# Residual halves side by side in one 512-column matmul, and weight sums formed by accumulating DMAs, in a seven-product SwiGLU stage

## The chip, the core and the metric

The kernel runs on one core of one Trainium2 chip. The metric is the device time of one launch in microseconds (us). The kernel before was run three times: 2362.85 us is the median, 2361.63 and 2367.12 the lowest and highest. A separate execution was recorded by the hardware profiler; it took 2364.33 us, of which 2362.6 us lie between the first and the last instruction (the span).

## The reference

The reference is one encoder layer over 512 tokens (two requests of 256), model width 2048: a mixing part (attention and a gated delta rule), a residual, and then a SwiGLU block whose inner width is 5632. The change touches the last line only, in the two products with `w_gate` and `w_up`:

```python
    h = h + mixed
    hn = rmsnorm(h, norm_ffn_w)
    return h + (jax.nn.silu(hn @ w_gate) * (hn @ w_up)) @ w_down
```

Everything is float32. The kernel gets that accuracy on TensorE by splitting each operand into a high part (rounded to float32r) and a low part (the rest), and adding three products: high weight with high activation, high weight with low activation, low weight with high activation.

## The kernel before

The gate and up products are computed with a seven-product scheme of Strassen's kind. The contraction (2048 rows) is cut in two halves, the 256 + 256 tokens are the two column halves, and two neighbouring blocks of 128 output columns are the two row halves. Seven sums of activation blocks (`A11, A12, S4, A22, S1, S2, S3`, 256 tokens each) are made once, ahead of the stage, for each of eight k-tiles (lines 846 to 857); `split` at line 857 writes their high parts to `XH[k]` and their low parts to `XL[k]`. On the weight side, sums of blocks are made for every block.

The stage is the loop at line 956: 22 pairs, each with one `block` of the gate weights and one of the up weights, so 44 calls of `block` (line 883). One call:

- loads four weight blocks of 128 x 1024 float32 (512 KB each) through SyncE's queue (`b11`, `b12` in a pool of their own for gate and for up, one buffer each; `b22`, `b21` in the three `raw` buffers);
- makes the sums of weights it needs with four VectorE operations (lines 905, 909, 915, 927);
- splits each of the seven weight operands (`w_split`, lines 874 to 878): ScalarE writes the high part `w_hi` (line 123), VectorE the low part `w_lo` (line 124), each in one of three rotating buffers;
- runs seven products (`product`, lines 866 to 872), each of 8 k-tiles times 3 matmuls of 256 columns;
- combines the products out of PSUM: ScalarE copies (lines 903, 913, 935), VectorE additions (919, 924, 925, 932), a multiplication by the reciprocal norm (937).

After an up block VectorE multiplies up and gate (963), and GpSimd's queue stores the result to `s_act` (971), which the last stage (`w_down`, 512-column matmuls throughout) loads again as `raw_a`.

Each engine works through its own instructions in a fixed order. The matmuls stay in program order. On the other engines a scheduler sets the order when the kernel is built; `ahead()` lets it place the weight splits some way ahead of the product that uses them.

The output columns of one `product` are half a PSUM bank, so products share banks: `pa` and `pc` hold two each.

Of the kernel before, what the change touches and what calls it, by code (L numbers as in the profile page):

```python
# [8 lines left out]
F32 = mybir.dt.float32  # L9
F32R = mybir.dt.float32r  # L10
I32 = mybir.dt.int32
AF = mybir.ActivationFunctionType
ALU = mybir.AluOpType
# [4 lines left out]
P = 128  # L18
T = 512
# [4 lines left out]
L = 256  # L24
# [29 lines left out]
def r32(ap):  # L54
    return ap.bitcast(F32)
# [3 lines left out]
def hybrid_encoder(ctx: ExitStack, tc: tile.TileContext, xT, w_in, w_ba, w_out, w_gate,  # L59
                   w_up, w_down, nw_mix, nw_ffn, nw_fin, na_bias, conv_w, lane_par,  # L60
                   dn_nw, y):
    nc = tc.nc
    act = nc.scalar.activation
    tt = nc.vector.tensor_tensor
# [5 lines left out]
    def mm(*a, **k):  # L70
        pin(nc.tensor.matmul(*a, **k))  # L71
# [6 lines left out]
    wp = ctx.enter_context(tc.tile_pool(name="wp", bufs=2, side="left"))  # L78
# [5 lines left out]
    pg = ctx.enter_context(tc.tile_pool(name="pg", bufs=3, space=PSUM))  # L84
# [35 lines left out]
    def split(hi, lo, src, scale=None):  # L120

        if scale is None:
            act(out=hi, in_=src, func=AF.Copy)  # L123
            tt(lo, src, r32(hi), ALU.subtract)  # L124
        else:
            act(out=hi, in_=src, func=AF.Copy, scale=scale)
            stt(lo, src, scale, r32(hi), ALU.mult, ALU.subtract)
# [50 lines left out]
    def half_gemm(ps, src, xs, start, stop, every=2):  # L178

        wh, wl = load_w(src, [8, P])  # L180
        for k in range(8):
            mm3(ps, wh[:, k], wl[:, k], xs[k][0], xs[k][1],
                start and k == 0, stop and k == 7)
            if k % every == every - 1:
                pump()
        advance(vector_work)

    def col_tile(src, xs):
        ps = pg.tile([P, T], F32, tag="g", name="ps_g")
        half_gemm(ps, src[0], xs[:8], True, False)  # L190
        half_gemm(ps, src[1], xs[8:], False, True)
        return ps
# [17 lines left out]
    psm = ctx.enter_context(tc.tile_pool(name="psm", bufs=3, space=PSUM))  # L210
    pso = ctx.enter_context(tc.tile_pool(name="pso", bufs=1, space=PSUM))
# [57 lines left out]
    for j in range(8):  # L269
        for k in (2 * j, 2 * j + 1):  # L270
            wh, wl = k0w[k // 8]
# [257 lines left out]
    for h in range(H):  # L529
        kq = wk.tile([P, 2, T], F32, tag="kq", bufs=2, name="kq")  # L530
        ps = ps_k0 if h == 0 else col_tile(w_in[2 * h], xs)
        conv_silu(ps, 8 + h, kq[:, 0])
        ps = ps_q0 if h == 0 else col_tile(w_in[2 * h + 1], xs)
# [62 lines left out]
    for h in range(H):  # L596
        ps = col_tile(w_in[16 + 3 * h], xs)
        qT = na.tile([P, T], F32, tag="qT", name="qT")
        stt(qT, ps, QSCALE, rstd, ALU.mult, ALU.mult)
        ps = col_tile(w_in[16 + 3 * h + 1], xs)  # L600
        kT = evac(ps, "kT", 1, na)
        ps = col_tile(w_in[16 + 3 * h + 2], xs)
# [168 lines left out]
    for h in range(H):  # L771
# [6 lines left out]
        ps = col_tile(w_in[40 + 2 * h], xs)  # L778
# [3 lines left out]
        ps = col_tile(w_in[40 + 2 * h + 1], xs)  # L782
# [29 lines left out]
    for i in pairs:  # L812
        ps = pg.tile([P, T], F32, tag="g", name="ps_g")
# [11 lines left out]

    hp_cm = tc.tile_pool(name="hp", bufs=1, side="right", reuse_waits="tile")
    hp = hp_cm.__enter__()
    XH = [hp.tile([P, 7, L], F32R, tag=f"xh{k}", name="xch") for k in range(8)]
    XL = [hp.tile([P, 7, L], F32R, tag=f"xl{k}", name="xcl") for k in range(8)]
    ga_cm = tc.tile_pool(name="gA", bufs=1, side="right", reuse_waits="tile")  # L830
    gA = ga_cm.__enter__()
    st_cm = tc.tile_pool(name="st", bufs=1, side="left", reuse_waits="tile")
# [2 lines left out]
    A11, A12, S4, A22, S1, S2, S3 = range(7)  # L835
    for n, i in enumerate(pairs):
        j = i % 8
        ps = pg.tile([P, T], F32, tag="g", name="ps_g")
        hk = st.tile([P, T], F32, tag="hk", bufs=2, name="hk")
        nc.sync.dma_start(hk, s_h1[i])  # L840
        half_gemm(ps, w_out[i, 1], dns, True, True)
        tt(hk, hk, ps, ALU.add)
        nc.gpsimd.dma_start(s_h2[i], hk)
        w = nwf[:, i:i + 1]
        if i < 8:
            cmb = st.tile([P, 7, L], F32, tag="cmb", name="cmb")
            a21 = st.tile([P, L], F32, tag="a21", name="a21")
            act(out=cmb[:, A11], in_=hk[:, :L], func=AF.Copy, scale=w)
            act(out=a21, in_=hk[:, L:], func=AF.Copy, scale=w)
            tt(cmb[:, S3], cmb[:, A11], a21, ALU.subtract)  # L850
        else:
            act(out=cmb[:, A12], in_=hk[:, :L], func=AF.Copy, scale=w)
            act(out=cmb[:, A22], in_=hk[:, L:], func=AF.Copy, scale=w)
            tt(cmb[:, S1], a21, cmb[:, A22], ALU.add)
            tt(cmb[:, S2], cmb[:, S1], cmb[:, A11], ALU.subtract)
            tt(cmb[:, S4], cmb[:, A12], cmb[:, S2], ALU.subtract)
            split(XH[j], XL[j], cmb)
        sq = acc if n == 0 else st.tile([P, T], F32, tag="sq", name="h_sq")
        act(out=sq, in_=hk, func=AF.Square)
        if n:  # L860
            tt(acc, acc, sq, ALU.add)
# [4 lines left out]
    def product(ps, w, c, first, done=False):  # L866

        wh, wl = w
        for k in range(8):
            for n, (u, x) in enumerate(((wh, XH), (wh, XL), (wl, XH))):  # L870
                mm(ps, u[:, k], x[k][:, c], start=(first and k == 0 and n == 0),
                   stop=(done and k == 7 and n == 2), skip_group_check=True)

    def w_split(src):
        hi = wp.tile([P, 8, P], F32R, tag="hi", bufs=3, name="w_hi")
        lo = wp.tile([P, 8, P], F32R, tag="lo", bufs=3, name="w_lo")
        split(hi, lo, src)
        return hi, lo

    def ahead():  # L880
        return tc.high_priority(offset=AHEAD)

    def block(src, f, pool, new_out, opened=None):

        with tc.high_priority(offset=3 * AHEAD):
            b11 = pool.tile([P, 8, P], F32, tag="b11", name="b11")
            b12 = pool.tile([P, 8, P], F32, tag="b12", name="b12")
            nc.sync.dma_start(b11, src[f, 0])
            nc.sync.dma_start(b12, src[f + 1, 0])
            b22 = wp.tile([P, 8, P], F32, tag="raw", bufs=3, name="b22")  # L890
            nc.sync.dma_start(b22, src[f + 1, 1])
            b21 = wp.tile([P, 8, P], F32, tag="raw", bufs=3, name="b21")
            nc.sync.dma_start(b21, src[f, 1])
        pa = pg.tile([P, T], F32, tag="g", name="ps_a")
        pc = psm.tile([P, T], F32, tag="s", name="ps_c")
        with ahead():
            w = w_split(b11)
        product(pa[:, :L], w, A11, True)
        if opened:
            opened()  # L900
        fp, out = state["fp"], new_out()
        p1 = fp.tile([P, L], F32, tag="p1", bufs=2, name="p1")
        nc.scalar.copy(p1, pa[:, :L])
        with ahead():
            tt(b11, b12, b11, ALU.subtract)
            w = w_split(b11)
        product(pc[:, L:], w, S1, True)
        with ahead():
            tt(b12, b22, b12, ALU.subtract)
            w = w_split(b12)  # L910
        product(pc[:, :L], w, S3, False)
        p75 = fp.tile([P, 2, L], F32, tag="p75", bufs=2, name="p75")
        nc.scalar.copy(p75, pc.rearrange("p (a t) -> p a t", a=2))
        with ahead():
            tt(b11, b22, b11, ALU.subtract)
            w = w_split(b11)
        product(pa[:, L:], w, S2, False)
        u2 = fp.tile([P, L], F32, tag="u2", bufs=2, name="u2")
        tt(u2, p1, pa[:, L:], ALU.add)
        with ahead():  # L920
            w = w_split(b22)
        product(pc[:, L:], w, S4, False, True)
        v = fp.tile([P, L], F32, tag="v", name="v")
        tt(v, u2, p75[:, 0], ALU.add)
        tt(out[:, 3], v, p75[:, 1], ALU.add)
        with ahead():
            tt(b11, b21, b11, ALU.subtract)
            w = w_split(b11)
        product(pc[:, :L], w, A22, False, True)
        with ahead():  # L930
            w = w_split(b21)
        tt(out[:, 1:3], pc.rearrange("p (a t) -> p a t", a=2),
           u2[:, None, :].broadcast_to([P, 2, L]), ALU.add)
        product(pa[:, :L], w, A12, False, True)
        nc.scalar.copy(out[:, 0], pa[:, :L])
        a = out.rearrange("p (f b) t -> p f (b t)", f=2)
        tt(a, a, rstd2[:, None, :].broadcast_to([P, 2, T]), ALU.mult)  # L937
        return out
# [17 lines left out]
    for p in range(NPAIR):  # L956
# [8 lines left out]
        if p // 2 == FIRST_SEG:  # L965
            k = p % 2 * 2
# [21 lines left out]
    fp = ctx.enter_context(tc.tile_pool(name="fq", bufs=2, side="left", reuse_waits="tile"))  # L988
# [174 lines left out]
```

## Time and profile before

| What | us |
|---|---|
| median of three runs | 2362.85 |
| the profiled execution, own time | 2364.33 |
| its span | 2362.6 |
| PE busy in the span | 2323.2 |
| VectorE busy | 1599.0 |
| ScalarE busy | 975.0 |
| GpSimd busy | 143.8 |
| the 20 loads of `raw_a` by GpSimd's queue, median from issue to landing | 4.6 |

In the profile PE is TensorE's matmul side, PEld its weight loads, DVE VectorE, ACT ScalarE, POOL GpSimd, SP SyncE, which issues DMAs. A row of a group has the line of the kernel, engine, operation, output and inputs, shape and count; then busy time, the mean of one in ns, and the idle time of the engine just before them with what ended it. A row of the timeline has start and duration in us and, in brackets, the idle time before it. A matmul's duration in the trace reaches from its start to the end of its pipeline, so that neighbours overlap; the distance from one start to the next is what counts for throughput.

### The profile page before, as it was taken

The page shows a single profiled execution, that of the slowest core. Times are in us where ns is not written, and L with a number is a line of the kernel's source. Part 1 is how long each engine was busy: PE and PEld are TensorE (multiplying, and loading weights), DVE is VectorE, ACT ScalarE, POOL GpSimd, SP SyncE. Part 2 cuts the span into 40 slices and gives each one's busy share as a digit, 9 for nine tenths or more (in the row PEclk, how much of TensorE's full clock was granted, in tenths as well). Part 3 has the DMA queues.
Part 4 walks back from the last instruction along what each step waited for, and adds up shares of the span by engine and source line. Part 5 has one row for each costly group of instructions (what it writes and reads, how often), then busy time and mean ns, then how long its engine had stood idle before and what let it go on. Part 6 is the DMA issues. An engine that isn't in the chain of part 4 may idle for free.

```text
span 2362.6 us, 35608 instructions
## 1 busy us (share of the span) xinstructions
PE 2323.2 (98%) x14500; PEld 2058.6 (87%) x14500; DVE 1599.0 (68%) x2164; ACT 975.0 (41%) x1464; POOL 143.8 (6%) x244
## 2 busy tenths in 40 slices
PE   8999999999999999899999999999999999999997
PEld 6777788877778788799999999999999888888887
DVE  7644699985566637788888888888888653422346
ACT  6777223324333315544444444444444331211125
POOL 2111200002100001000000000000000110000000
PEclk9999999999999999999999999999999999999999
DMA  5434623346434546333333333333333563423332
GB/s 202 130 116 132 161 93 103 95 120 179 145 115 125 212 157 208 120 115 119 116 126 117 126 117 119 114 121 113 118 106 99 192 227 98 133 93 97 98 125 72
DMA packets 88980, 305.30 MB, mean 129 GB/s; under 512 B 11776, under 2 KB 16288, under 8 KB 87664
## 3 DMA queue, kind: packets, MB, share of 16 engines
q1 hardware_dynamic: 71392, 245.67, 32.5%
q0 software_dynamic: 17424, 57.36, 8.0%
q8 instruction: 114, 1.87, 0.3%
q14 instruction: 50, 0.41, 0.1%
HBM read 266.98 MB, written 36.00 MB: 128 GB/s over the span
## 4 chain that ended last, share of the span: by engine, by line
PE 57%; DVE 0%; DMA 0%; issue 0%; ACT 0%; POOL 0%; DVEq 0%
PE ps_c L71 21%; PE ps_a L71 16%; PE ps_g L71 11%; PE ps_s L71 9%; DMA raw_a<-s_act 0%; DVE hT L1043 0%; DVE w_lo L124 0%; DVE up L937 0%; ACT w_hi L123 0%; ACT aq L123 0%; DVE up L963 0%; DVE hT L1010 0%; DVE dgs L1037 0%; POOL s_act L971 0%; DVE ssq_acc L1060 0%
## 5 line engine op out<-in xcount | busy, mean ns | idle before, releaser
L123 ACT ACTIVATE w_hi<-b 128x1024 fp32r<-128x1024 f32 x308 | 327.0, 1062 | 490.9 <-PE ps_c L71 164.6
L124 DVE TENSOR_TENSOR w_lo<-w_raw,w_hi 128x1024 fp32r<-128x1024 f32 x224 | 274.1, 1224 | 277.9 <-ACT w_hi L123 273.9
L124 DVE TENSOR_TENSOR w_lo<-b,w_hi 128x1024 fp32r<-128x1024 f32 x308 | 376.3, 1222 | 120.3 <-ACT w_hi L123 120.3
L123 ACT ACTIVATE w_hi<-w_raw 128x1024 fp32r<-128x1024 f32 x224 | 236.8, 1058 | 487.0 <-PE ps_s L71 278.2
L71 PE MATMUL ps_c<-xch,w_hi 128*128 128x256 f32 x1408 | 399.9, 284 | 0.0
L71 PE MATMUL ps_c<-xcl,w_hi 128*128 128x256 f32 x1408 | 399.0, 283 | 0.0
L71 PE MATMUL ps_c<-xch,w_lo 128*128 128x256 f32 x1408 | 399.0, 283 | 0.0
L71 PE MATMUL ps_g<-xhi,w_hi 128*128 128x512 f32 x896 | 369.6, 412 | 0.0
L71 PE MATMUL ps_g<-xhi,w_lo 128*128 128x512 f32 x896 | 351.6, 392 | 6.6 <-DVE w_lo L124 6.6
L71 PE MATMUL ps_g<-xlo,w_hi 128*128 128x512 f32 x896 | 350.8, 392 | 0.0
L71 PE MATMUL ps_a<-xch,w_hi 128*128 128x256 f32 x1056 | 299.0, 283 | 5.3 <-ACT xch L123 4.0
L71 PE MATMUL ps_a<-xcl,w_hi 128*128 128x256 f32 x1056 | 299.1, 283 | 1.7 <-DVE xcl L124 1.7
L71 PE MATMUL ps_a<-xch,w_lo 128*128 128x256 f32 x1056 | 299.0, 283 | 0.0
L71 PEld LDWEIGHTS ps_c<-xch,w_hi 128*128 128x128 f32 x1408 | 271.0, 192 | 0.5 <-issue 0.5
L71 PEld LDWEIGHTS ps_c<-xcl,w_hi 128*128 128x128 f32 x1408 | 271.0, 192 | 0.5 <-issue 0.5
L71 PEld LDWEIGHTS ps_c<-xch,w_lo 128*128 128x128 f32 x1408 | 270.9, 192 | 0.0
L71 PEld LDWEIGHTS ps_g<-xhi,w_lo 128*128 128x128 f32 x896 | 168.8, 188 | 46.0 <-DVE w_lo L124 9.1
L71 PEld LDWEIGHTS ps_a<-xch,w_hi 128*128 128x128 f32 x1056 | 202.7, 192 | 5.7 <-ACT xch L123 4.2
L71 PEld LDWEIGHTS ps_g<-xhi,w_hi 128*128 128x128 f32 x896 | 169.0, 189 | 43.1 <-issue 7.4
L71 PEld LDWEIGHTS ps_a<-xcl,w_hi 128*128 128x128 f32 x1056 | 202.8, 192 | 1.9 <-DVE xcl L124 1.9
L71 PEld LDWEIGHTS ps_a<-xch,w_lo 128*128 128x128 f32 x1056 | 202.9, 192 | 0.0
L71 PEld LDWEIGHTS ps_g<-xlo,w_hi 128*128 128x128 f32 x896 | 169.3, 189 | 30.9 <-issue 0.2
(307 smaller groups left out, 3468.7 us busy)
## 6 DMA issues: line engine op xcount, KB each, us to landing
w_raw<-in_w_in_dram SPq DMA_DIRECT2D x112, 512.0 KB, 3.6
b<-in_w_gate_dram SPq DMA_DIRECT2D x88, 512.0 KB, 3.5
b<-in_w_up_dram SPq DMA_DIRECT2D x88, 512.0 KB, 3.5
w_raw<-in_w_down_dram SPq DMA_DIRECT2D x88, 512.0 KB, 3.5
w_raw<-in_w_out_dram SPq DMA_DIRECT2D x32, 512.0 KB, 3.6
s_act<-up POOLq DMA_DIRECT2D x20, 512.0 KB, 2.9
raw_a<-s_act POOLq DMA_DIRECT2D x20, 512.0 KB, 4.6
qg<-s_eg SPq DMA_DIRECT2D x8, 1024.0 KB, 4.6
```

The source lines that it names most:

```text
L71: pin(nc.tensor.matmul(*a, **k))
L123: act(out=hi, in_=src, func=AF.Copy)
L124: tt(lo, src, r32(hi), ALU.subtract)
```

## The change

The high and low parts of an activation sum now lie side by side in one tile, `XC[k]` of shape 7 x 2 x 256. A k-tile takes two matmuls in place of three: the high weight against the 512 columns of high and low together, and the low weight against the 256 columns of high. A product therefore fills a whole bank with two halves that are added when it is read. Four banks are in use for a block (`pa`, `pb`, `pc`, `pd`).

The weight sums are no longer made on VectorE. Two signs on the activation side are turned, so that every weight sum is an addition, and the block in `first` is added to in place three times: by DMAs on GpSimd's queue that add a block from memory to what is in SBUF. `second` gets one such addition. The order of the products is A11, S3, S1, A12, S2, S4, A22; `first` is the weight of the 1st, 3rd, 5th and 7th, `second` of the 2nd, and plain loads (`b21`, `b22`) of the 4th and 6th.

```diff
-    XH = [hp.tile([P, 7, L], F32R, tag=f"xh{k}", name="xch") for k in range(8)]
-    XL = [hp.tile([P, 7, L], F32R, tag=f"xl{k}", name="xcl") for k in range(8)]
+    XC = [hp.tile([P, 7, 2, L], F32R, tag=f"xc{k}", name="xc") for k in range(8)]
...
-            tt(cmb[:, S1], a21, cmb[:, A22], ALU.add)
+            tt(cmb[:, S1], a21, cmb[:, A22], ALU.subtract)
             tt(cmb[:, S2], cmb[:, S1], cmb[:, A11], ALU.subtract)
-            tt(cmb[:, S4], cmb[:, A12], cmb[:, S2], ALU.subtract)
-            split(XH[j], XL[j], cmb)
+            tt(cmb[:, S4], cmb[:, A12], cmb[:, S2], ALU.add)
+            split(XC[j][:, :, 0], XC[j][:, :, 1], cmb)
...
         for k in range(8):
-            for n, (u, x) in enumerate(((wh, XH), (wh, XL), (wl, XH))):
-                mm(ps, u[:, k], x[k][:, c], start=(first and k == 0 and n == 0),
-                   stop=(done and k == 7 and n == 2), skip_group_check=True)
+            mm(ps, wh[:, k], XC[k][:, c], start=(first and k == 0), stop=False,
+               skip_group_check=True)
+            mm(ps[:, 0], wl[:, k], XC[k][:, c, 0], start=False, stop=(done and k == 7),
+               skip_group_check=True)
+
+    def plus_both(out, a, ps, op=ALU.add):
+
+        if a is None:
+            nc.scalar.copy(out, ps[:, 1])
+            tt(out, out, ps[:, 0], ALU.add)
+        else:
+            tt(out, ps[:, 0], a, op)
+            tt(out, out, ps[:, 1], ALU.add)
...
+    def plus(dst, src):
+
+        nc.gpsimd.dma_start(dst, src, accum_op=ALU.add)
...
+            first = pool.tile([P, 8, P], F32, tag="first", name="w_first")
+            nc.sync.dma_start(first, src[f, 0])
+            second = pool.tile([P, 8, P], F32, tag="second", name="w_second")
+            nc.sync.dma_start(second, src[f + 1, 0])
+            plus(second, src[f + 1, 1])
...
         with ahead():
-            w = w_split(b11)
-        product(pa[:, :L], w, A11, True)
+            w = w_split(first)
+            plus(first, src[f + 1, 0])
+        product(pa, w, A11, True)
...
-        nc.scalar.copy(p1, pa[:, :L])
+        plus_both(p1, None, pa)
         with ahead():
-            tt(b11, b12, b11, ALU.subtract)
-            w = w_split(b11)
-        product(pc[:, L:], w, S1, True)
+            w = w_split(second)
+        product(pc, w, S3, True)
+        p7 = fp.tile([P, 2, L], F32, tag="p7", name="p7")
+        nc.scalar.copy(p7, pc)
         with ahead():
-            tt(b12, b22, b12, ALU.subtract)
-            w = w_split(b12)
-        product(pc[:, :L], w, S3, False)
...
+            w = w_split(first)
+            plus(first, src[f + 1, 1])
+        product(pd, w, S1, True)
+        d = fp.tile([P, 2, L], F32, tag="d", name="d")
+        tt(d, pd, p7, ALU.subtract)
+        with ahead():
+            w = w_split(b21)
+        product(pa, w, A12, False, True)
+        plus_both(out[:, 0], None, pa)
+        with ahead():
+            w = w_split(first)
+            plus(first, src[f, 1])
+        product(pb, w, S2, True, True)
+        u2 = fp.tile([P, L], F32, tag="u2", name="u2")
+        plus_both(u2, p1, pb)
+        tt(out[:, 3], d[:, 0], u2, ALU.subtract)
+        tt(out[:, 3], out[:, 3], d[:, 1], ALU.add)
         with ahead():
             w = w_split(b22)
-        product(pc[:, L:], w, S4, False, True)
...
+        product(pd, w, S4, False, True)
+        plus_both(out[:, 2], u2, pd, ALU.subtract)
...
         with ahead():
+            w = w_split(first)
+        product(pc, w, A22, False, True)
+        plus_both(out[:, 1], u2, pc)
         a = out.rearrange("p (f b) t -> p f (b t)", f=2)
```

More of the change, by code (lines that the diff above doesn't have):

```diff
@@ L881, in ahead, with bank @@
         return tc.high_priority(offset=AHEAD)
+    def plus(dst, src):
+        nc.gpsimd.dma_start(dst, src, accum_op=ALU.add)
     def block(src, f, pool, new_out, opened=None):
         with tc.high_priority(offset=3 * AHEAD):
[L886 to L889, printed above, removed]
+            first = pool.tile([P, 8, P], F32, tag="first", name="w_first")
[3 more added lines that the diff above has]
+            plus(second, src[f + 1, 1])
+            b21 = wp.tile([P, 8, P], F32, tag="raw", bufs=3, name="b21")
+            nc.sync.dma_start(b21, src[f, 1])
             b22 = wp.tile([P, 8, P], F32, tag="raw", bufs=3, name="b22")
             nc.sync.dma_start(b22, src[f + 1, 1])
[L892 to L895, printed above, removed]
+        def bank(pool_, tag, nm):
+            return pool_.tile([P, T], F32, tag=tag, name=nm).rearrange("p (a t) -> p a t", a=2)
+        pa, pb = bank(pg, "g", "ps_a"), bank(pso, "o0", "ps_b")
+        pc, pd = bank(psm, "s", "ps_c"), bank(pso, "o1", "ps_d")
         with ahead():
-            w = w_split(b11)
-        product(pa[:, :L], w, A11, True)
+            w = w_split(first)
+            plus(first, src[f + 1, 0])
+        product(pa, w, A11, True)
         if opened:
@@ L901, in block @@
         fp, out = state["fp"], new_out()
-        p1 = fp.tile([P, L], F32, tag="p1", bufs=2, name="p1")
-        nc.scalar.copy(p1, pa[:, :L])
+        p1 = fp.tile([P, L], F32, tag="p1", name="p1")
+        plus_both(p1, None, pa)
         with ahead():
-            tt(b11, b12, b11, ALU.subtract)
-            w = w_split(b11)
-        product(pc[:, L:], w, S1, True)
+            w = w_split(second)
+        product(pc, w, S3, True)
+        p7 = fp.tile([P, 2, L], F32, tag="p7", name="p7")
+        nc.scalar.copy(p7, pc)
@@ L908, in block @@
         with ahead():
-            tt(b12, b22, b12, ALU.subtract)
-            w = w_split(b12)
-        product(pc[:, :L], w, S3, False)
-        p75 = fp.tile([P, 2, L], F32, tag="p75", bufs=2, name="p75")
-        nc.scalar.copy(p75, pc.rearrange("p (a t) -> p a t", a=2))
-        with ahead():
[L915 to L919, printed above, removed]
+            w = w_split(first)
@@ L920, in block @@
+        tt(out[:, 3], d[:, 0], u2, ALU.subtract)
+        tt(out[:, 3], out[:, 3], d[:, 1], ALU.add)
         with ahead():
             w = w_split(b22)
-        product(pc[:, L:], w, S4, False, True)
-        v = fp.tile([P, L], F32, tag="v", name="v")
-        tt(v, u2, p75[:, 0], ALU.add)
-        tt(out[:, 3], v, p75[:, 1], ALU.add)
+        product(pd, w, S4, False, True)
+        plus_both(out[:, 2], u2, pd, ALU.subtract)
         with ahead():
-            tt(b11, b21, b11, ALU.subtract)
-            w = w_split(b11)
@@ L929, in block @@
[L929 to L935, printed above, removed]
+            w = w_split(first)
+        product(pc, w, A22, False, True)
+        plus_both(out[:, 1], u2, pc)
         a = out.rearrange("p (f b) t -> p f (b t)", f=2)
```

## The prediction

> **What bounds the kernel now.** I read the page first: its busy times, slices and the shares of the chain of waits.
>
> ```profile
> span 2362.6 us, 35608 instructions
> ...
> PE 2323.2 (98%) x14500; PEld 2058.6 (87%) x14500; DVE 1599.0 (68%) x2164; ACT 975.0 (41%) x1464; POOL 143.8 (6%) x244
> ...
> DMA  5434623346434546333333333333333563423332
> ...
> PE 57%; DVE 0%; DMA 0%; issue 0%; ACT 0%; POOL 0%; DVEq 0%
> ```
>
> TensorE is busy for 98% of the span, and the chain runs through its matmuls. The changed stage lies in slices 17 to 32, where the DMA engines are at some three tenths. So I looked at a stretch inside it, with the table by windows (busy us of each engine, granted clock, DMA share, GB/s), and at the chain in order of time (start, duration, count).
>
> ```profile
> 1200.00:1600.00 400.00, 400.00 (x3336) 400.00 (x3335) 327.15 (x328) 177.02 (x208) 5.33 (x10) 1.00 0.37 119
> ```
>
> ```profile
> 1005.66 2.88 PE ps_a L71 x24
> 1008.54 5.76 PE ps_c L71 x48
> 1014.30 5.76 PE ps_a L71 x48
> 1020.06 5.76 PE ps_c L71 x48
> 1025.82 2.88 PE ps_a L71 x24
> ...
> 1896.32 2.72 PE ps_s L71 x12
> 1899.04 2.72 PE ps_g L71 x12
> ```
>
> One product (24 matmuls of 256 columns) takes 2.88 us, 120 ns each, without a gap, and a block 1025.82 - 1005.66 = 20.16 us, 7 products. The last rows are from the final stage: there 12 matmuls of 512 columns take 2.72 us, 226.7 ns each. VectorE is 82% busy beside it, ScalarE 44%. The weights are ready in time, as the timeline shows:
>
> ```profile
> 1207.17 1.06 ACT L123 ACTIVATE w_hi<-b 128x1024 fp32r<-128x1024 f32 x1 [1.82 <-PE ps_c L71]
> 1208.27 1.22 DVE L124 TENSOR_TENSOR w_lo<-b,w_hi 128x1024 fp32r<-128x1024 f32 x1 [1.65 <-ACT w_hi L123]
> ```
>
> ScalarE's split waits for PE: it has no free buffer until an older product ends. With three buffers it stands two products ahead of its use.
>
> **The matmuls.** A k-tile costs 3 x 120 = 360 ns now and 226.7 + 120 = 346.7 ns after: the columns are the same 768, and one fixed cost of 13.3 ns goes (226.7 is 2 x 120 less 13.3). There are 44 x 7 x 8 = 2464 k-tiles, so 32.9 us, if nothing else holds TensorE: a block would take 7 x 8 x 346.7 ns = 19.41 us. That the mixed pair keeps these paces is not shown; the bounds are 333.3 ns (a second 13.3 ns gone, 65.7 us) and 360 ns (nothing gained). Neither end counts in the forecast, since the loop below is longer.
>
> The Trainium skill speaks against the gain here (TensorE: Matmul & The Clock Gate, Back-to-back issue gap): it gives a gap of N / 2.4 + 2.5 ns, 109.2 and 215.8 ns, by which a dropped matmul saves 2.5 ns, some 6 us in all (an estimate from that page). The rows have 120 and 226.7 ns, so I go by them.
>
> **VectorE and ScalarE.** Four sums of weights leave VectorE in each block:
>
> ```profile
> L905 DVE TENSOR_TENSOR b<-b,b 128x1024 f32<-128x1024 f32 x44 | 53.9, 1226 | 1.5
> L915 DVE TENSOR_TENSOR b<-b,b 128x1024 f32<-128x1024 f32 x44 | 53.9, 1225 | 1.5
> L927 DVE TENSOR_TENSOR b<-b,b 128x1024 f32<-128x1024 f32 x44 | 53.8, 1224 | 0.8
> L909 DVE TENSOR_TENSOR b<-b,b 128x1024 f32<-128x1024 f32 x44 | 53.5, 1216 | 0.0
> L919 DVE TENSOR_TENSOR u<-p,ps_a 128x256 f32<-128x256 f32 x44 | 18.5, 421 | 30.6 <-PE ps_a L71 30.6
> ```
>
> That is 4.89 us. The halves cost ten operations of 256 columns in place of three, 7 x 0.42 = 2.95 us more; one of 512 columns stays. VectorE ends 1.9 us lighter, and ScalarE keeps its three copies. Neither becomes the bound: off the path, no cost in the sum. The activation sums are split once, in another layout: nothing.
>
> **The accumulating DMAs.** This is the part that decides. A sum that stood on VectorE for 1.2 us now needs a DMA that can start only when the split before it has read `first`, and the next split of `first` can start only when it has landed. In the built order of the changed kernel VectorE works in each block as follows (L881 and the like left out; the number is the product):
>
> ```
> lo 7 (previous block), lo 1, lo 2, additions for products 6 and 7 of the previous block,
> rstd, [up x gate], lo 3, lo 4, additions, lo 5, lo 6, additions, lo 7, lo 1 (next block)
> ```
>
> So there is a loop, once around per block, and each link is a true dependence or the order of one engine: lo 7 of the last block, lo 1 right behind it, DMA, hi 3, lo 3, DMA, hi 5, lo 5, DMA, hi 7, lo 7. That `first` has two buffers (gate and up) doesn't open it, because lo 1 stands behind lo 7 in VectorE's queue. Behind a waiting hi 3 on ScalarE stand hi 4 and the copies of products 1 and 2; behind the first DMA on GpSimd's queue stand the addition to `second` and, every second block, the store to `s_act`.
>
> The trace of before has such a loop with plain DMAs, at the start of the last stage, where `raw_a` is loaded by GpSimd's queue into a buffer that a split frees:
>
> ```profile
> 1903.09 0.53 POOL L995 DMA_DIRECT2D raw_a<-s_act  x1 [2.34 <-DVE aq L124]
> ...
> 1907.10 1.06 ACT L123 ACTIVATE ar<-raw_a 128x1024 fp32r<-128x1024 f32 x1 [1.55 <-DMA raw_a<-s_act]
> ...
> 1908.19 1.23 DVE L124 TENSOR_TENSOR ar<-raw_a,ar 128x1024 fp32r<-128x1024 f32 x1 [0.79 <-ACT ar L123]
> ...
> 1909.72 0.53 POOL L995 DMA_DIRECT2D raw_a<-s_act  x1 [2.08 <-DVE ar L124]
> ```
>
> One round: 4.01 us from the issue to ScalarE's start, 2.32 us to the end of the low part (1909.42), 0.30 us to the next issue. Call the first term a. Its spread for twelve loads around these, the table by windows for that stretch, and issues from the page's list of DMAs (KB each, median us to landing):
>
> ```profile
> DMA to landing us min/median/max: 3.7/3.9/5.1
> ...
> 1895.00:1935.00 40.00, 40.00 (x177) 32.81 (x176) 26.44 (x28) 19.24 (x19) 6.14 (x12) 1.00 0.68 220
> ...
> b<-in_w_gate_dram SPq DMA_DIRECT2D x88, 512.0 KB, 3.5
> ...
> s_act<-up POOLq DMA_DIRECT2D x20, 512.0 KB, 2.9
> ...
> s_h<-h POOLq DMA_DIRECT2D x16, 256.0 KB, 2.3
> ```
>
> A plain 512 KB load by this queue: shortest 3.7, median 3.9, longest 5.1; a loop pays the mean, and I take 4.1. The DMA load will be alike: 8 transfers of weights a block and half a store, 4 of them with a second operand, against 4.5 transfers at a share of 0.37 now, so 0.37 x 20.16 / 4.5 = 1.66 us of all engines for each and 12.5 x 1.66 = 20.7 us in a block of some 25 us at the heaviest, 14.1 us at the lightest, a share of 0.56 to 0.83.
>
> An accumulation also fetches the old contents from SBUF. No row has one. Below, it costs as little as SyncE's loads, a = 3.5 (a transfer with more to do can't well beat them); above, it is two transfers end to end, a = 8.2. For the middle I take the price of more bytes out of SBUF: the stores of 512 and of 256 KB differ by 0.6 us, so 512 KB more is 1.2 us, a = 4.1 + 1.2 = 5.3. It is nearest to what happens: the same queue, one completion, twice the bytes read.
>
> The Trainium skill (DMA: Bandwidth & Descriptors, Rules for kernel authors) says that an accumulating DMA reads its destination and writes it later, and that the next access has to wait for its semaphore. Its price for this queue (Anatomy of one DMA) is 2.0 us + bytes / 436 GB/s: 3.2 us for 512 KB, where the row has 3.7 at the least, and 4.4 us for twice the bytes; with 4.4 in the loop, as an estimate from that page, the time would be 2452 us.
>
> **The sum.** Two low parts back to back on VectorE stand 1.14 us apart:
>
> ```profile
> 1210.70 0.43 DVE L924 TENSOR_TENSOR v<-u,p 128x256 f32<-128x256 f32 x1
> 1211.16 0.42 DVE L925 TENSOR_TENSOR up<-v,p 128x256 f32<-128x256 f32 x1
> ...
> 1221.69 1.22 DVE L937 TENSOR_TENSOR up<-up,rstd 128x1024 f32<-128x1024 f32 x1
> 1222.83 1.22 DVE L124 TENSOR_TENSOR w_lo<-b,w_hi 128x1024 fp32r<-128x1024 f32 x1
> ```
>
> The loop is 1.14 + 3 x (2.32 + 0.30 + a) = 9.0 + 3a. With a = 5.3 it is 24.9 us, longer than the products' 19.41 us, so it sets the block, and TensorE waits ahead of products 3, 5 and 7. Against 20.16 us that is 4.74 us more, 209 us over 44 blocks: span 2362.6 + 209 = 2571. The profiled execution took 2364.33 and the median of the runs is 2362.85, so the forecast for the median is 2571 us as well. Each microsecond of a is worth 3 x 44 = 132 us.
>
> **The rivals.**
> - *Hidden accumulation, faster.* The loop equals the old block at 9.0 + 3a = 20.16, a = 3.72, and vanishes behind the matmuls at a = 3.47. With a = 3.5 it is 19.5 us; in gate blocks a second path counts, from lo 7: product 7 itself at 2.77 us, three additions at 0.46, rstd and up x gate at 1.14 each, lo 3 at 1.22, two more rounds of 6.12, and it gives 19.9 us from one lo 7 to the next (0.46 and 1.14 us are the distances of neighbouring starts). Mean 19.7: 2362.6 - 0.46 x 44 = 2342 us. For it: SyncE's loads land after 3.5 us, and the share of DMA is low. Against: GpSimd's plain loads need 3.7 at the least. The skill's 3.2 us, if the old contents cost nothing, would be on this side.
> - *No surcharge.* The addition is hidden in the transfer, a = 4.1: 21.3 us a block, 50 us more, 2413 us.
> - *Two transfers in one.* The destination is read first, with its own latency, a = 8.2: 33.6 us a block, 591 us more, 2954 us. Queueing behind the SyncE loads pushes the same way.
> - *The matmuls don't gain.* Should the mixed pair still take 360 ns, the 32.9 us aren't there; beside the loop that changes nothing, and with hidden sums the time stays near 2363 us.
>
> **How the numbers follow.** I give the forecast (a from 4.5 to 6.5) 0.55, no surcharge (3.8 to 4.5) 0.17, two transfers or heavy queueing (over 6.5) 0.15, hidden accumulation 0.13, of which 0.10 is faster by over 0.2%, and 0.03 within 0.2%, about what runs of this kernel can tell from no change. Slower: 0.87. The range reaches from a = 3.93 (2390) to a = 7.4 (2850); it leaves out the hidden case and the tail of the heavy one, about 0.19.
>
> **What would show it.** In the profile after: TensorE idle in the stage, with idle time ahead of ps_c or ps_d, ps_b and the second use of ps_c (products 3, 5, 7) and none ahead of 2, 4, 6; ScalarE's high parts of `first` waiting for the DMA; GpSimd's `first` rows with a landing near 5 us; a block near 25 us and products that run in 8 x 346.7 ns = 2.77 us between the waits; VectorE below 65% in the stage. It is wrong if the landing is under 3.7 us, if TensorE has no gaps, or if GpSimd's queue itself is late because the addition to `second` holds those to `first` behind it.

## The result, and the profile after

| | us |
|---|---|
| before, median of four runs | 2363.91 (2361.63 to 2367.12) |
| after, median of four runs | 2859.67 (2852.58 to 2860.63) |
| ratio | 1.209, 95% interval 1.2065 to 1.2114 |
| span of the profiled execution after | 2858.3 |

The kernel became 496 us slower. The direction was predicted, but the time is 289 us above the forecast and 10 us above the range. Page of after: span, busy times, queues (packets, MB, share of 16 engines), landings.

```profile
span 2858.3 us, 31183 instructions
...
PE 2506.2 (88%) x12036; PEld 2040.3 (71%) x12036; DVE 1508.8 (53%) x2296; ACT 952.3 (33%) x1464; POOL 296.7 (10%) x420
...
q0 software_dynamic: 42768, 149.64, 25.3%
q1 hardware_dynamic: 71392, 245.67, 24.9%
...
w_first<-in_w_gate_dram POOLq DMA_DIRECT2D x66, 512.0 KB, 8.0
w_first<-in_w_up_dram POOLq DMA_DIRECT2D x66, 512.0 KB, 7.7
b<-in_w_gate_dram SPq DMA_DIRECT2D x44, 512.0 KB, 5.9
```

The additions to `first` land after 8.0 and 7.7 us where 5.3 had been taken, and SyncE's loads after 5.9 where they needed 3.5. No engine is full. The windows and the waits of the stretch that was read before show why TensorE stands (total wait, times, longest):

```profile
1200.00:1600.00 400.00, 305.06 (x1377) 247.00 (x1377) 178.86 (x242) 106.14 (x132) 45.74 (x55) 0.85 0.57 137
```

```profile
ACT w_hi L123 <- DMA w_first<-in_w_up_dram: 144.0, 19, 9.6
...
ACT w_hi L123 <- DMA w_first<-in_w_gate_dram: 130.2, 15, 10.4
POOL w_second L894 <- DMA w_second<-in_w_up_dram: 50.0, 6, 8.6
POOL w_second L894 <- DMA w_second<-in_w_gate_dram: 47.8, 6, 8.5
```

ScalarE's high parts of `first` wait for the additions for 274 of 400 us. The two lower rows are a wait that the prediction did not have: GpSimd's queue itself stands for 98 us, with the addition to `second` at its head, until SyncE's load of `second` has landed. One block (of the up weights) in the timeline (start, duration, idle time before):

```profile
1503.46 2.36 DVE L124 TENSOR_TENSOR w_lo<-w_first,w_hi 128x1024 fp32r<-128x1024 f32 x2 [0.18 <-ACT w_hi L123]
...
1506.11 0.86 POOL L894 DMA_DIRECT2D w_first<-in_w_up_dram  x1 [8.63 <-DVE w_lo L124]
...
1506.98 0.33 SPq L903 DMA_DIRECT2D w_second<-in_w_up_dram  x1
...
1514.47 1.06 ACT L123 ACTIVATE w_hi<-w_first 128x1024 fp32r<-128x1024 f32 x1 [8.78 <-DMA w_first<-in_w_up_dram]
1515.07 0.86 POOL L894 DMA_DIRECT2D w_second<-in_w_up_dram  x1 [8.09 <-DMA w_second<-in_w_up_dram]
...
1517.07 0.87 POOL L894 DMA_DIRECT2D w_first<-in_w_up_dram  x1 [1.14 <-DVE w_lo L124]
...
1525.08 1.06 ACT L123 ACTIVATE w_hi<-w_first 128x1024 fp32r<-128x1024 f32 x1 [6.92 <-DMA w_first<-in_w_up_dram]
...
1527.69 0.87 POOL L894 DMA_DIRECT2D w_first<-in_w_up_dram  x1 [9.75 <-DVE w_lo L124]
...
1533.55 2.00 ACT L123 ACTIVATE w_hi<-w_first 128x1024 fp32r<-128x1024 f32 x2 [6.20 <-DMA w_first<-in_w_up_dram]
...
1534.64 2.36 DVE L124 TENSOR_TENSOR w_lo<-w_first,w_hi 128x1024 fp32r<-128x1024 f32 x2 [2.96 <-ACT w_hi L123]
```

Lo 7 and lo 1 stand back to back at 1503.46 and again at 1534.64: a block of 31.18 us. The three terms a (issue to ScalarE's start) are 1514.47 - 1506.11 = 8.36, 8.01 and 5.86 us. The formula gives 9.0 + 22.23 = 31.2 us: the loop is the predicted one, only a is larger. By the timeline, two transfers lie in the way of the first two. SyncE's load of `second` starts 0.87 us behind the first addition, and both are late (8.4 and 8.1 us). That late load releases the addition to `second`, which goes out 2.00 us ahead of the second addition to `first`. It does not hold that one back in the queue (it goes out some 0.3 us behind its low part, as predicted); it is the transfer that takes longer. The third has the engines nearly to itself. Over the 18 blocks from 1100 to 1700 us the three take 8.4, 8.9 and 6.0 us on average. In gate blocks the store to `s_act` goes out between the addition to `second` and the second one to `first`, and that one takes 9.7 us, against 8.1 in up blocks. Windows of 2 us show the DMA share in these bursts (last but one column):

```profile
1508.00:1510.00 2.00, 2.00 (x13) 1.75 (x12) 1.94 (x4) 0.00 (x0) 0.00 (x0) 1.00 1.01 178
...
1514.00:1516.00 2.00, 0.42 (x1) 0.19 (x1) 0.45 (x1) 1.53 (x2) 0.86 (x1) 0.98 0.00 0
...
1520.00:1522.00 2.00, 2.00 (x7) 1.71 (x7) 0.00 (x0) 0.00 (x0) 0.00 (x0) 0.50 1.04 231
```

A mean share of 0.57 is all 16 engines full for some 5 us, then nothing while the split runs, then full again.

### The profile page after: what moved, and what is told of

Read it like the earlier page. It is cut to its first block, busy times and chain, and to the rows that moved or that the text cites. A ratio compares the mean times of both kernels' runs of the same rounds, so it can differ in the third digit from the quotient of the medians.

```text
span 2858.3 us, 31183 instructions
## 1 busy us (share of the span) xinstructions
PE 2506.2 (88%) x12036; PEld 2040.3 (71%) x12036; DVE 1508.8 (53%) x2296; ACT 952.3 (33%) x1464; POOL 296.7 (10%) x420
## 3 DMA queue, kind: packets, MB, share of 16 engines
q0 software_dynamic: 42768, 149.64, 25.3%
q1 hardware_dynamic: 71392, 245.67, 24.9%
## 5 line engine op out<-in xcount | busy, mean ns | idle before, releaser
L123 ACT ACTIVATE w_hi<-w_first 128x1024 fp32r<-128x1024 f32 x176 | 181.5, 1054 | 1002.9 <-DMA w_first<-in_w_up_dram 465.2
L124 DVE TENSOR_TENSOR w_lo<-w_first,w_hi 128x1024 fp32r<-128x1024 f32 x176 | 211.9, 1224 | 474.9 <-ACT w_hi L123 474.8
L71 PE MATMUL ps_d<-xc,w_hi 128*128 128x512 f32 x704 | 306.4, 462 | 87.5 <-ACT w_hi L123 87.5
L71 PE MATMUL ps_b<-xc,w_hi 128*128 128x512 f32 x352 | 191.6, 555 | 123.8 <-ACT w_hi L123 123.8
L71 PE MATMUL ps_c<-xc,w_hi 128*128 128x512 f32 x704 | 269.8, 417 | 17.5 <-ACT w_hi L123 17.2
L71 PE MATMUL ps_a<-xc,w_hi 128*128 128x512 f32 x704 | 257.7, 404 | 7.9 <-DVE xc L124 5.3
L71 PE MATMUL ps_d<-xc,w_lo 128*128 128x256 f32 x704 | 228.2, 324 | 29.5 <-DVE w_lo L124 29.5
L71 PE MATMUL ps_c<-xc,w_lo 128*128 128x256 f32 x704 | 208.9, 297 | 26.3 <-DVE w_lo L124 26.3
L71 PE MATMUL ps_a<-xc,w_lo 128*128 128x256 f32 x704 | 199.5, 283 | 0.0
L71 PEld LDWEIGHTS ps_d<-xc,w_lo 128*128 128x128 f32 x704 | 160.0, 227 | 43.1 <-DVE w_lo L124 43.1
```

## Experiments

Theory at the start: an undisturbed addition costs 5.3 us as predicted, and the rest comes from transfers that share the engines at the wrong moment, above all the addition to `second`. Rival: an accumulating DMA simply costs about 8 us. From each time below a mean a is worked out: block = 20.16 + (time - 2363) / 44, a = (block - 9.0) / 3.

### The price of one addition by itself

A small program with nothing of the layer in it: sections of ten dependent rounds, each with one or two transfers by GpSimd's queue (plain or adding), with none, one or two loads by SyncE beside them.

```diff
+        for _ in range(N):
+            for t in s:
+                nc.sync.dma_start(t, block(w_up))
+            for t in a:
...
+                if accumulate:
+                    nc.gpsimd.dma_start(dst, src, accum_op=ALU.add)
+                else:
+                    nc.gpsimd.dma_start(dst, src)
```

> A small program that computes nothing of the layer (it writes a tile of its own to the outputs): chains of ten DMAs of weight blocks into one SBUF tile, each released by a short VectorE copy that has read the last one, first plain, then accumulating, then accumulating 256 KB, then accumulating beside one and beside two plain 512 KB loads of SyncE's queue issued at the same moment, plain beside two loads, and last two accumulations, and two plain loads, at once. In the changed kernel an accumulation of 512 KB took 5.2 us to landing at its quickest kinds (second) and 8.0 us for first; its packets kept the 16 engines for 3.0 us against 1.5 us of a plain load. Theory (shared engines): landing is a fixed part near 2.2 us and the engine time of all that is issued together: plain 3.7, accumulating 5.2, half size 3.7, beside one load 6.7, beside two 8.2, plain beside two 6.7, two accumulations at once 8.2. Rival (the accumulation itself is slow and irregular): near 8 us alone already, and no more than 1 us added by the loads.

Its table of DMA issues (count, KB, median us to landing; "accu" adds, and in "ld" SyncE loads beside it):

```profile
accu_ld_acc<-in_w_gate_dram POOLq DMA_DIRECT2D x20, 512.0 KB, 7.9
...
plain_acc<-in_w_gate_dram POOLq DMA_DIRECT2D x10, 512.0 KB, 3.6
accu_acc<-in_w_gate_dram POOLq DMA_DIRECT2D x10, 512.0 KB, 5.4
plain_ld_acc<-in_w_gate_dram POOLq DMA_DIRECT2D x10, 512.0 KB, 5.8
```

Alone, an addition lands after 5.4 us and a plain load after 3.6; beside one or two of SyncE's loads an addition takes 7.9, beside two a plain load 5.8. The plain one beside two loads came sooner than expected (6.7). The rival falls: 8 us is the price in company.

### Plain loads in place of the additions

The four DMAs overwrite and add nothing; order and bytes out of memory stay.

```diff
-        nc.gpsimd.dma_start(dst, src, accum_op=ALU.add)
+        nc.gpsimd.dma_start(dst, src)
```

> The changed kernel with each accumulating DMA as a plain one of the same bytes on the same queue, in the same place (so the sums of weights are left out, a block replaces what was in the tile). Loop of a block: 9.0 us and the three times from issue to ScalarE's start. Theory (landing = 2.2 us and the engine time of all that is in flight, 1.5 us for each plain transfer): 5.5 to 6.7, 5.7 and 4.4 us, 16.2 in all, a block of 25.2 us, about 2585 us, range 2520 to 2640. Rival A (the accumulating operation itself is slow, the other transfers don't matter): 4.1 us each, 21.3 us a block, 2413 us. Rival B (it is GpSimd's queue that is slow here): no change, 2860 us.

2645.43 us (2643.41 to 2647.45), ratio 1.1185 (1.1152 to 1.1217), a = 5.9. More was left than expected: 282 of the 496 us stay without any addition. The timeline of GpSimd's queue:

```profile
1513.19 0.53 POOL L894 DMA_DIRECT2D w_second<-in_w_gate_dram  x1 [6.88 <-DMA w_second<-in_w_gate_dram]
1513.71 0.54 POOL L989 DMA_DIRECT2D s_act<-up  x1
1515.16 0.53 POOL L894 DMA_DIRECT2D w_first<-in_w_gate_dram  x1 [0.91 <-DVE w_lo L124]
1526.65 0.53 POOL L894 DMA_DIRECT2D w_first<-in_w_gate_dram  x1 [10.96 <-DVE w_lo L124]
```

With the transfer to `second` and the store 1.5 to 2 us ahead, the second DMA needs 8.9 us until ScalarE starts (at 1524.04); the next one, with none ahead of it, 4.0 (1530.63). Those 4.0 us are the prediction's plain a of 4.1. So position costs plain transfers dearly too.

### The sum for `second` on VectorE

Three additions a block stay; the fourth sum becomes a VectorE operation.

```diff
-            plus(second, src[f + 1, 1])
...
+            tt(second, second, b22, ALU.add)
             w = w_split(second)
```

> The changed kernel with only the sum in second made by VectorE from the loaded b22 (one accumulating DMA of four goes; VectorE has 1.14 us more a block). Theory (shared engines): the second accumulation to first is no longer issued 2 us behind another one of 3.0 us engine time, its time falls from 8 to 9 us to about 6; the loop falls by 2 to 3 us, 90 to 130 us in all, 2730 to 2770 us. Rival (each accumulation slow by itself): the loop has the same three, 2860 us.

2612.34 us (2611.17 to 2613.51), ratio 1.1045 (1.1013 to 1.1077), a = 5.6: 118 us below the expectation. Timeline, one block:

```profile
1513.19 0.86 POOL L894 DMA_DIRECT2D w_first<-in_w_up_dram  x1 [8.51 <-DVE w_lo L124]
1521.39 0.87 POOL L894 DMA_DIRECT2D w_first<-in_w_up_dram  x1 [7.34 <-DVE w_lo L124]
1529.36 0.86 POOL L894 DMA_DIRECT2D w_first<-in_w_up_dram  x1 [7.10 <-DVE w_lo L124]
```

ScalarE starts at 1518.78, 1526.76 and 1534.84, so a is 5.6, 5.4 and 5.5 (5.9, 5.4 and 5.5 on average from 1100 to 1700 us): with one addition of four gone, the other three have nearly the price of the small program. The expectation had left them more than half of their delay. SyncE's load of `second` is still there, 2.0 us behind the first addition (at 1515.18) where it was 0.87; no run moves this load alone, so what it costs by itself is not shown.

### The addition to `second` behind the others

All four additions stay, but GpSimd's order is fixed: the addition to `second` goes out behind the third one to `first`, the store behind the second.

```diff
-        nc.gpsimd.dma_start(dst, src, accum_op=ALU.add)
+        pin(nc.gpsimd.dma_start(dst, src, accum_op=ALU.add))
...
         product(pd, w, S1, True)
+        if late:
+            late()
```

> The changed kernel with all its accumulating DMAs, only their order on GpSimd's queue set by hand: the addition to second of the next block after the third addition to first of this one, not between the first and the second, and the store of up x gate behind the second. Theory (the loss beyond the forecast comes from the addition to second, which goes 2 us ahead of the second addition to first and fills the engines): the three times fall from 8.4, 8.0 and 5.9 us to 5.3 to 6.3 us as in the run without that addition and with narrow matmuls, a block of 25.5 to 27.5 us, 2600 to 2690 us. Rival (the sum of bytes in flight decides, wherever they stand): the bytes are the same, 2830 to 2870 us.

2657.23 us (2648.44 to 2659.31), ratio 1.123 (1.1208 to 1.1253), a = 5.95. Windows, and the page's landings:

```profile
1200.00:1600.00 400.00, 333.40 (x1675) 271.12 (x1673) 213.43 (x292) 125.64 (x154) 56.25 (x68) 0.94 0.72 168
```

```profile
w_first<-in_w_gate_dram POOLq DMA_DIRECT2D x66, 512.0 KB, 5.5
```

At a higher share of the engines (0.72 against 0.57) the same additions to `first` land in 5.5 us (median) in place of 8: not the number of bytes in flight is at fault but their order. The lateness has moved to the addition to `second`, which now lands after 9.1 and 8.9 us (gate, up) where it took 5.3, but ScalarE waits for it only 22 of 400 us. The first addition of a block still takes 6.6 us on average, the others 5.6. This order, of the addition to `second` and of the store, is worth 2859.67 - 2657.23 = 202 us; no run moves one of the two alone.

### Three narrow matmuls again, with the DMAs of the change

```diff
-            mm(ps, wh[:, k], XC[k][:, c], start=(first and k == 0), stop=False,
+            mm(ps[:, 0], wh[:, k], XC[k][:, c, 0], start=(first and k == 0), stop=False,
+               skip_group_check=True)
+            mm(ps[:, 1], wh[:, k], XC[k][:, c, 1], start=False, stop=False,
                skip_group_check=True)
```

> The changed kernel with its matmuls as before: three of 256 columns for a k-tile in place of one of 512 and one of 256, into the same halves; DMAs and VectorE as in the changed kernel. Theory (the loop of accumulations sets the block): within 15 us of 2860. Rival (the wide matmul, its banks or the halves carry part of the loss): it differs by at least the matmuls' own 33 us, or falls towards 2363.

A miss: 2679.05 us (2676.78 to 2681.32), ratio 1.1327 (1.1294 to 1.136). Not the matmuls helped. With other matmuls the scheduler built another order on GpSimd's queue, as the timeline shows:

```profile
1520.16 0.87 POOL L896 DMA_DIRECT2D w_first<-in_w_gate_dram  x1 [10.42 <-DVE w_lo L124]
1528.43 0.87 POOL L896 DMA_DIRECT2D w_first<-in_w_gate_dram  x1 [7.41 <-DVE w_lo L124]
1528.97 1.23 POOL L896 DMA_DIRECT2D w_second<-in_w_gate_dram  x1
```

The addition to `second` now stands behind the second one to `first` instead of ahead of it, and the three a of this block are 5.7, 5.5 and 6.1 us (ScalarE at 1525.82, 1533.93, 1542.62). By accident it is much the same as the experiment above, and it says nothing on the matmul.

### The sums without DMAs

First all four sums as VectorE operations, with the product for S1 in the second place:

```diff
-        nc.gpsimd.dma_start(dst, src, accum_op=ALU.add)
+        nc.vector.tensor_tensor(dst, dst, src, ALU.add)
...
+            add(first, second)
+            w = w_split(first)
+        product(pd, w, S1, True)
+        with ahead():
+            add(second, b22)
             w = w_split(second)
```

> One part of the change alone: the 512-column matmuls and the halves as in the changed kernel, but the four sums of weights on VectorE from loaded blocks (product order A11, S1, S3, A12, S2, S4, A22), no accumulating DMA. VectorE has per block 7 low parts, 4 sums, rstd and half of up x gate at 1.14 us and additions of some 4.6 us, 18.9 us, beside 19.41 us of matmuls. Theory (all of the loss comes from the accumulating DMAs, the matmuls gain 13.3 ns for each k-tile): 2330 to 2365, likeliest 2345, short waits on VectorE taking part of the 33 us. Rival (the wide form or its two additions for each product carry a loss of their own): over 2380.

2404.9 us (2402.05 to 2406.6), ratio 1.0169 (1.0154 to 1.0184): the rival's side. Its group by line in the stretch from 1200 to 1600 us, and the timeline ahead of one second product:

```profile
L71 PE MATMUL ps_d<-xc,w_hi 128*128 128x512 f32 x304 | 109.5, 400 | 20.9 <-ACT w_hi L123 20.9
```

```profile
1396.15 1.06 ACT L123 ACTIVATE w_hi<-w_first 128x1024 fp32r<-128x1024 f32 x1 [2.84 <-DVE w_first L894]
...
1400.56 1.06 ACT L123 ACTIVATE w_hi<-b 128x1024 fp32r<-128x1024 f32 x1 [1.71 <-PE ps_a L71]
1401.16 0.41 DVE L881 TENSOR_TENSOR up<-up,ps_d 128x256 f32<-128x256 f32 x1
...
1401.72 0.47 PE L71 MATMUL ps_d<-xc,w_hi 128*128 128x512 f32 x1 [1.13 <-ACT w_hi L123]
```

TensorE stands 20.9 us of 400, 1.1 us a block, ahead of the second product. The profile puts the wait down to ScalarE's high part, but the one for this product, which did wait for its sum, is done at 1397.21, 4.5 us before. The high part that ends at 1401.62 belongs to product 4. What the second product needs and gets last is its PSUM bank: VectorE reads product 6 of the block before out of `ps_d` until 1401.57, and the matmul starts 0.15 us later. The expectation of the run with a third tile, below, takes the sum for the cause.

Then the same sums on GpSimd (`nc.gpsimd.tensor_tensor`):

> As the last one, with the four sums on GpSimd as tensor additions in place of VectorE. The duration of such an addition of 128 x 1024 is in no trace so far. The loop through first is 1.14 + 3 x (2.62 + the addition); below 3.4 us for it the matmuls set the block: 2330 to 2340 if GpSimd adds in 2 us and disturbs nobody. Rival: GpSimd takes 3.5 us or more, or VectorE's own instructions get longer beside it: over 2365.

2484.37 us (2479.19 to 2485.59), ratio 1.0499 (1.0481 to 1.0517). Timings of the line in its trace (ns: shortest, median, longest):

```profile
L894 POOL TENSOR_TENSOR w_first<-w_first,b x88: 2351/2414/3470, 969.6 to 1973.2; 128x1024 f32<-128x1024 f32 x88
```

A sum takes 2.4 us, twice VectorE's 1.22, but by the expectation's own loop, 1.14 + 3 x (2.62 + 2.41) = 16.2 us, this would be hidden. It is the second half of the rival that came true: VectorE's operations beside a GpSimd addition get longer. In the stretch from 1200 to 1600 us the low part of `second` takes 2.86 us on average where it took 1.22 with the sums on VectorE, line 944 2.50 in place of 0.42, and 37 of the 39 us that TensorE stands there are waits for VectorE.

And with the three sums of `first` on VectorE, the one of `second` by an accumulating DMA:

```diff
-            add(second, b22)
+            nc.gpsimd.dma_start(second, src[f + 1, 1], accum_op=ALU.add)
```

> As the run with all sums on VectorE, but the sum in second by an accumulating DMA (one a block, outside the loop through first), so that VectorE has 1.14 us less, 17.8 us a block. Theory (an accumulating DMA costs only where the next split waits for it in the loop): the matmuls set the block, 2330 to 2345 us, faster than both kernels. Rival (each accumulating DMA costs, hidden or not, for instance through late loads): over 2365.

A miss: 2412.04 us (2411.39 to 2416.13), ratio 1.0204 (1.0189 to 1.0219). The addition overwrites `second`, so it waits for the sum that reads it, and it is in the chain again. The waits of the stretch:

```profile
ACT w_hi L123 <- DVE w_first L894: 54.0, 19, 2.8
...
ACT w_hi L123 <- DMA w_second<-in_w_up_dram: 44.9, 9, 5.7
ACT w_hi L123 <- DMA w_second<-in_w_gate_dram: 42.8, 9, 4.9
```

### A third tile, and another bank

The first sum goes into a tile of its own, so that it needs only loads:

```diff
+        third = fp.tile([P, 8, P], F32, tag="third", name="w_third")
...
-            add(first, second)
-            w = w_split(first)
+            add(third, first, second)
+            w = w_split(third)
```

> The 512-column matmul with the four sums on VectorE as in the run with all sums there, but the sum for S1 (second product) goes into a third tile, so that it needs the loads alone and not the low part of the product before. Theory: that run lost its 1.1 us a block because ScalarE's high part of S1 waited for a sum that stood on VectorE behind u2; with the wait gone a block is 20.8 - 1.1 = 19.7 us, 0.46 us less than the 20.16 us before, 20 us over 44 blocks: 2343 us, from 2335 to 2364 (VectorE has some 18.7 us of work a block, 95%, which may give a part of it back). Rival: VectorE is simply too full, at 18.7 us of work any order leaves waits of about 1 us: 2385 to 2410.

2403.9 us (2399.64 to 2404.78), ratio 1.0162 (1.0147 to 1.0177): a miss, no gain. ScalarE's wait for the sum (54.0 of 400 us before) is gone, and TensorE's wait ahead of product 2 is as it was, now under its own name. Timeline:

```profile
1302.39 0.47 PE L71 MATMUL ps_d<-xc,w_hi 128*128 128x512 f32 x1 [0.99 <-DVE ga L881]
1323.35 0.47 PE L71 MATMUL ps_d<-xc,w_hi 128*128 128x512 f32 x1 [0.95 <-DVE up L881]
```

Product 2 writes the bank of product 6 of the block before, which VectorE has not read yet; the matmul again starts 0.15 us behind that read. With two of the sums moved to GpSimd:

```diff
+            add(third, first, second, nc.gpsimd)
...
+            add(second, second, b22, nc.gpsimd)
```

> As the run with the third tile, and two of the four sums (S1's into the third tile and S3's into second) on GpSimd, which took 2.4 to 2.5 us for one in the run with all sums there. They need loads and low parts that are done long before, so their length should be hidden; VectorE has 16.3 us of work a block. Theory: no wait ahead of TensorE, a block of 19.4 to 19.8 us: 2330 to 2350 us. Rival: two GpSimd additions in a row (5 us) come too late for product 2 or 3 because the third tile is only free after the last low part of the block before, and the wait is in the chain again: 2380 to 2480.

2393.34 us (2392.05 to 2394.66), ratio 1.0119 (1.0102 to 1.0136): the rival's time, but not its reason. ScalarE waits 18 of 400 us for one of GpSimd's sums, TensorE for none. VectorE's groups by form:

```profile
L124 DVE TENSOR_TENSOR w_lo<-w_first,w_hi 128x1024 fp32r<-128x1024 f32 x20 | 44.5, 2223 | 1.8 <-ACT w_hi L123 0.6
L944 DVE TENSOR_TENSOR ga<-d,u 128x256 f32<-128x256 f32 x10 | 26.2, 2625 | 0.0
```

Line 944 takes 2.62 us where it took 0.42 with the sums on VectorE, the low part 2.22 in place of 1.22: they meet a GpSimd addition. VectorE is busy for 385 of 400 us, it reads product 1 too late in every second block, and TensorE waits for that ahead of product 4. Last, the third tile with all sums on VectorE again, and products 2 and 6 in the pool that has three banks:

```diff
-        pc, pd = bank(psm, "s", "ps_c"), bank(pso, "o1", "ps_d")
+        pc, pd = bank(pso, "o1", "ps_c"), bank(psm, "s", "ps_d")
```

> The run with the third tile, with two PSUM tiles exchanged: products 2 and 6 (ps_d) take the pool with three banks, products 3 and 7 (ps_c) the single bank. In the run with the third tile TensorE waits 0.97 us ahead of product 2 in every block, because VectorE has not yet read product 6 of the block before out of the one bank. Theory: that wait is all that is left; product 3 starts 2.8 us later and finds its bank read, so a block is 20.7 - 0.97 = 19.75 us, 0.4 us less than before: 2345 us, from 2335 to 2362. Rival: VectorE with some 18.7 us of work a block is itself late, and another wait of about the same size takes the place of this one: 2385 to 2405.

2343.13 us (2338.39 to 2356.75; two of the six runs took over 2355, why is open), ratio 0.9928 (0.9904 to 0.9953): 0.7% faster than the kernel before. Its windows and the chain of waits:

```profile
1200.00:1600.00 400.00, 400.00 (x2310) 352.69 (x2309) 380.17 (x484) 184.36 (x218) 5.33 (x10) 1.00 0.36 122
```

```profile
1218.05 2.77 PE ps_a L71 x16
...
1237.46 2.77 PE ps_a L71 x16
```

TensorE has no gap, and a block is 1237.46 - 1218.05 = 19.41 us, although VectorE is 95% busy. The exchange of banks without the third tile was not tried, so whether the tile is needed stays open.

## Why the prediction was right or wrong

**What bounds the kernel, and the loop: right.** The loop, its order, the fixed 9.0 us and TensorE idle ahead of products 3, 5 and 7 are all in the trace. The total agrees as well: 496 us over 44 blocks make a block of 31.4 us and a = 7.5, and 2.18 us over the forecast's 5.3 at 132 us for each is the 289 us that were missing. The prediction's rival of heavy queueing (a over 6.5) is where the time fell; it had been put together with two transfers end to end, at 0.15.

**The step that failed: the term a, taken as 5.3 for all three additions.** 5.3 is the price of an undisturbed one (5.4 alone, 5.6 with the addition to `second` gone). The prediction named the addition to `second` on GpSimd's queue, but feared only that it would hold the queue, which it does not; as a transfer in company with the second addition to `first` it put it at nothing, and SyncE's load of `second`, which releases it, as well. In place of 5.3 us the three took 8.4, 8.9 and 6.0. The runs divide the 289 us: 202 for the position of the addition to `second` (with the store's), 2657.23 - 2612.34 = 45 for its presence at a better place (moving it to VectorE also takes its traffic away), and 2612.34 - 2571 = 41 for a price of the undisturbed one that was 0.3 us too small.

**The surcharge.** 1.2 us came from the bytes of two stores. The small program has 5.4 - 3.6 = 1.8 us for the same bytes, and in the layer 5.5 us (additions, with the fourth sum on VectorE) stand against 4.0 (plain): 1.5. That 5.3 came so near to 5.4 is in part luck, since the 4.1 under it was too high for the small program. "No surcharge" and "two transfers end to end" (8.2 us each) both fall; the time near the second of them came about in another way, by queueing.

**The share of the engines.** A share of 0.56 to 0.83 was expected and 0.57 measured, and it was used as if transfers met at random. Here they don't: the loop issues them in bursts, and a load that one addition delays releases the next transfer in its way.

**The matmuls: right, and hidden.** 8 x 346.7 ns = 2.77 us a product and 19.41 us a block are what the last experiment has to the digit. The Trainium skill (TensorE: Matmul & The Clock Gate, Back-to-back issue gap) gives the formula that the prediction used for a single matmul by itself and not for a stream; by it a product would take 8 x 325 ns = 2.60 us, an estimate from that page. The measurement decides for the rows. The sign that products run in 2.77 us between the waits holds for part of them only: product 3 of the block above, at a granted clock of 0.50, took 6.1 us from its first matmul to the next product's (1515.58 to 1521.70), 0.74 of them waiting for its low part. Of the 32.9 us, 21 came in that run; its one long wait, 7.7 us ahead of the first S1 product, is one part of the rest.

**VectorE.** Its lighter load counted for nothing beside the loop, as predicted. With the sums left on VectorE it is what stands in the way: with some 18.6 us of work in a block, it reads one PSUM bank too late or in time, and that decides between 1.7% slower and 0.7% faster; the third tile alone changed nothing.

Not tried: `second` in two buffers, so that its load comes early, and additions spread over several smaller DMAs.

## What to carry to other kernels

A DMA in a loop of dependences has to be priced by its latency in the company it will have: look what its queue issues ahead of it, and which late load releases that. A mean share of the DMA engines says little where the transfers come in bursts. Before an engine's work is moved to DMAs, try the gain without them: here it was had with one more tile and an exchange of PSUM banks. And where the profile names the releaser of a wait, look when the thing that the waiting instruction really needs was done: the high part named in the run with all sums on VectorE was another product's, and the bank was the cause.

## What the runs showed of the hardware

An addition holds the 16 engines about twice as long as a plain load, by an estimate from the queues. Those of before:

```profile
q1 hardware_dynamic: 71392, 245.67, 32.5%
q0 software_dynamic: 17424, 57.36, 8.0%
```

q0 took 25.3% of 2858.3 us less 8.0% of 2362.6, 534 us, for the 176 additions: 3.03 us of all 16 engines each. SyncE's loads took 24.9% of 2858.3, 712 us, for 245.67 MB: 1.52 us for 512 KB. GpSimd also needs 0.86 us to issue one, against 0.53.

A VectorE operation with two SBUF inputs that meets a GpSimd addition takes until that is over, 2.62 us in place of 0.42: in the run with two sums on GpSimd one lasts from 1311.33 to 1313.95, the addition from 1310.40 to 1313.65. One that reads a PSUM bank kept its 0.42 us beside an addition (at 1308.08). The Trainium skill (SBUF — State Buffer, SBUF: two separate sides) has this rule: the two engines share a pair of ports that one holds for a whole instruction, also against a VectorE operation with two SBUF inputs if the GpSimd one reads SBUF. The rows agree: line 944 reads two SBUF tiles.

After a wait TensorE ran at a granted clock of 0.50 for some us (the window from 1520 to 1522 of after), but not after every wait (1.00 from 1528 to 1530); it costs little there, as the loop is longer.
